# Decay of a chunked state-space scan: eight exponentials made one, bias and bound moved to GpSimd, mask moved to the cross products

## The chip, the cores and the metric

The kernel runs on one core of a Trainium2 chip. The metric is the device time of one execution in microseconds, as the median of several runs. The core has a matrix engine (TensorE, PE in the profile, whose weight loads are shown apart as PEld), a vector engine (VectorE, DVE), an engine for activation functions (ScalarE, ACT), a general engine (GpSimd, POOL) and an engine that issues transfers (SyncE, SP). Each works off its own queue in order and they meet at semaphores. PE writes its results to PSUM; the other data of the core lie in SBUF.

## The reference, cut to what matters

The reference is one layer of a streaming encoder: 1024 prompt positions and 64 sample positions go through a combined input projection, a state-space scan (SSD), differential attention, gated branches and a convolutional feed-forward part. The change lies in the scan. For one chunk, with `dtc` the step sizes, `bc` and `cc` the two projected factors and `xc` the rows, the reference computes:

```python
acum = jnp.cumsum(dtc * a_neg, axis=1)
seg = acum[:, :, None] - acum[:, None, :]
decay = jnp.exp(jnp.where(causal[None, :, :, None, None], seg, -jnp.inf))
xdt = xc * dtc[..., None]
cb = jnp.einsum('blgn,bsgn->blsg', cc, bc)
y = jnp.einsum('blsg,blsge,bsgep->blgep', cb, decay, xdt)
y = y + jnp.einsum('blgn,bgepn->blgep', cc, state) * jnp.exp(acum)[..., None]
to_end = jnp.exp(acum[:, -1:] - acum)
state = state * jnp.exp(acum[:, -1])[..., None, None] + jnp.einsum('blgn,blge,blgep->bgepn', bc, to_end, xdt)
```

There are 32 heads in 4 groups of 8. The decay differs by head (`e`), the cross products `cb` are shared by the 8 heads of a group. `a_neg` is negative, so `seg` is at most zero on the causal side.

## The kernel before, in words

The kernel holds all 1088 positions as columns and goes through these stages: input projections, attention with the rest of the input projections between its steps, the scan with branch products between its steps, the last branch product, the output projection, and the feed-forward part. The order in which each engine's queue is filled is made by a planner: the program is traced in one order, every instruction has a priority from that order, and the planner gives each engine the instruction of highest priority that it expects to be ready, by a simulated timeline of its own. Some instructions are pinned behind others by hand (`issue_after`) or raised (`high_priority`), but not those of the scan's steps.

**The step sizes** are made early, in `steps()`, while the q and k projections run. `dt_tok` is the step size, `nacum` the negative running sum of `dt * a`, `dtw` the step size times the decay to the chunk's end, each as a tile of 128 positions by 9 chunks by 32 heads. `dt_tok` and `dtw` are the two halves of one tile `dtt`. The running sums are also written, head by head as rows, to the scratch `a_sc` in DRAM.

**The scan** goes over 36 steps: 4 groups, and 9 chunks in each, 8 of 128 positions (the kernel uses 128 where the reference uses 64, which gives the same sums) and one of 64 for the sample stream. A step is cut into `front` and `back`, and `front` of the next step is traced ahead of `back` of this one. `ask` (L1284) loads the running sums of 8 heads, broadcast to all partitions, into the tile `bc` of 128 x 8 x 128; there are four such buffers.

`front` works in this order:

- ACT takes the exponential of `bc` into `e2` (L1294), twice, for the term from the old state.
- PE transposes the rows into `tr` (L1297) and makes the cross products in `cb` (L1299, L1300); ACT copies `cb` to SBUF as `b_cb` (L1302), the transposed factor in its first 128 columns and the cross products behind it.
- DVE multiplies `tr` by the two halves of `dtt` into `xx` (L1306), of which `xdt` and `xw` are the halves.
- POOL masks `bc`: it puts -1e30 where the column is before the row's position (L1307).
- ACT takes the exponential of `bc` head by head (L1309), eight instructions, since the bias `nacum` is one number per partition and head.
- DVE multiplies `bc` by the cross products (L1310).

`back` multiplies `xdt` by `bc` into `yi` on PE (L1318), the old state into `ye` (L1324); DVE joins them in `y` (L1325, L1326). PE makes the update of the state (L1330) from `b_cb` and `xw`; POOL multiplies the old state by its decay (L1335) and DVE adds the update (L1337). After each span of 384 or 320 columns `gated`, `normed` and `scaled` (L1342 to L1374) gate and normalise `y` on DVE and ACT and store it.

**Between the steps** the function `fill` traces branch products, 1.17 units a step, which keep PE's queue full: weights are loaded, cast on ACT (L155), the remainder taken on DVE (L156), three matmuls a block run on PE (L170 to L172), and the result is copied out of one of three PSUM banks (`more = psi, 1` and the two of `pm`) by ACT (L232, L970) or DVE (L234). None of these depends on the step beside which it is traced.

Of the kernel before, what the change touches and what calls it, by code (L numbers as in the profile page):

```python
# [11 lines left out]
AF = mybir.ActivationFunctionType  # L12
ALU = mybir.AluOpType
# [4 lines left out]
P = 128  # L18
# [71 lines left out]
def hybrid_layer(ctx: ExitStack, tc: tile.TileContext, xT, xt, prm, cst, rope, wvd, win, wbs, wba, wout, wup, wdn,  # L90
                 ckT, cv, st0, yT, kT, v, ssm, conv, ffn):
    nc = tc.nc
    V, S, G, PE = nc.vector, nc.scalar, nc.gpsimd, nc.tensor
    act = S.activation
# [166 lines left out]
    nacum, decs = (dq.tile([P, 9, 32], F32, name=n) for n in ("nacum", "decs"))  # L261
    dtt = dq.tile([P, 2, 9, 32], F32, name="dtt")
    dt_tok, dtw = dtt[:, 0], dtt[:, 1]
# [441 lines left out]
    def steps():  # L705
        flat = [four[:, 288 * i : 288 * (i + 1)] for i in range(3)] + [row("fx", "dt2")[:, :288]]
        da, e, t, t2 = (x.rearrange("p (a b) -> p a b", b=32) for x in flat)
# [30 lines left out]
        V.tensor_tensor(out=flat(dtw), in0=pl, in1=flat(nacum), op=ALU.add)  # L738
        act(dtw, dtw, AF.Exp)
        V.tensor_tensor(out=dtw, in0=dtw, in1=dt_tok, op=ALU.mult)  # L740
        yield
        for c, w in WIDE:
            af = row("fc", "af")[:32, :w]
# [176 lines left out]
    for at, (p, s) in enumerate(rest):  # L920
# [8 lines left out]
        if s == 1 and p in LATER:  # L929
            split_part(LATER[p], seen["copy"], seen["read"])  # L930
    beside = chain(cached_keys(), one_by_one(steps()))
    for n in range(1, len(INPUT)):
        blocks = blocks_of(n + 1) if n + 1 < len(INPUT) else None
# [331 lines left out]
    with (tc.tile_pool(name="sin", bufs=1) as sin, tc.tile_pool(name="sp", bufs=1) as sp,  # L1265
# [21 lines left out]
        def front(g, ch, o, bx, xs, bc):  # L1287
            L = P if ch < 8 else TS
            cs = slice(o, o + L)
            h8 = slice(8 * g, 8 * g + 8)  # L1290
            e2 = sp.tile([P, 4, P], F32, name="e2", tag="e2", bufs=3)
            for u in range(2):
                half = slice(64 * u, 64 * u + 64)
                act(e2[half, :, :L], bc.rearrange("p (j u) t -> p u j t", u=2)[half, u, :, :L], AF.Exp)  # L1294
            tr = psi.tile([P, 512], F32, name="tr", tag="tr")
            for j in range(4):
                PE.transpose(tr[:L, P * j : P * (j + 1)], xs[:, j, cs], ident)  # L1297
            cb = psi.tile([P, 512], F32, name="cb", tag="cb")
            PE.transpose(cb[:L, 0:P], bx[:, 0, cs], ident)  # L1299
            PE.matmul(cb[:L, P : P + L], bx[:, 0, cs], bx[:, 1, cs], start=True, stop=True)  # L1300
            b_cb = sp.tile([P, 2 * P], F32, name="b_cb", tag="b_cb", bufs=3)
            S.copy(b_cb[:L, : P + L], cb[:L, : P + L])  # L1302
            xx = sp.tile([P, 2, 8, 64], F32, name="xx", tag="xx", bufs=2)
            xdt, xw = xx[:, 0], xx[:, 1]
            tr3 = tr[:L].rearrange("p (e q) -> p e q", e=8).unsqueeze(1).to_broadcast([L, 2, 8, 64])
            V.tensor_tensor(out=xx[:L], in0=tr3, in1=dtt[:L, :, ch, h8].unsqueeze(3).to_broadcast([L, 2, 8, 64]), op=ALU.mult)  # L1306
            G.affine_select(bc[:L, :, :L], bc[:L, :, :L], [[0, 8], [1, L]], ALU.is_ge, -1e30, base=0, channel_multiplier=-1)  # L1307
            for e in range(8):
                act(bc[:L, e, :L], bc[:L, e, :L], AF.Exp, bias=nacum[:L, ch, 8 * g + e : 8 * g + e + 1])  # L1309
            V.tensor_tensor(out=bc[:L, :, :L], in0=bc[:L, :, :L], in1=b_cb[:L, P : P + L].unsqueeze(1).to_broadcast([L, 8, L]), op=ALU.mult)  # L1310
            return L, cs, bc, e2, b_cb, xdt, xw

# [65 lines left out]
        def scan():  # L1378
# [9 lines left out]
            def begin(n):  # L1388
                if n == len(steps):
                    return None  # L1390
                if n and n + 2 < len(steps):
                    asked.append(ask(*steps[n + 2]))
                i, g, c, w, o = steps[n]
                return front(g, (c + o) // P, o, *got[i], asked[n])
# [465 lines left out]
    for i in range(4 * len(DOWN)):  # L1860
        g, last = i // 4, i % 4 == 3 and i + 1 < 4 * len(DOWN)
# [125 lines left out]
```

## Time and profile before

| | us |
|---|---|
| median of 3 runs | 2413.91 |
| lowest and highest of them | 2413.68, 2415.92 |
| the profiled execution, its own time | 2411.51 |
| its span in the trace | 2409.7 |
| PE busy | 2373.4 |
| DVE busy | 1729.4 |
| ACT busy | 1201.2 |
| POOL busy | 634.4 |
| first scan step's `bc` product (L1310) starts at | 1136.3 |
| last scan step's `bc` product starts at | 1456.7 |

The profile is of one execution, taken on the core itself. The table's busy times are sums over the whole span. The granted clock of TensorE was 0.999 over the span. A row that groups instructions reads: line, engine, operation, tile written and tiles read, shapes, how many; then busy microseconds and mean nanoseconds of one; then the idle time of the engine ahead of them and whom it waited for. A row of the timeline reads: start, duration, engine, line, and how many instructions are merged in it. A row of waits reads: who waited, for whom, microseconds in all, how many times, the longest. Durations of matmuls overlap, since PE works on several at once, and spans on POOL are rough.

### The profile page before, as it was taken

The numbers are of one execution on the slowest core, as the hardware profiler recorded it, in microseconds if no ns is written. First come the engines' busy times: TensorE is split into PE (matmuls) and PEld (weight loads), VectorE is DVE, ScalarE is ACT, GpSimd is POOL, SyncE is SP. The second block draws the span as 40 slices with busy tenths as digits, with TensorE's granted clock in tenths as the row PEclk, the third lists the DMA queues.
The fourth block names the chain that finished last, engine by engine and source line by source line (L and its number), as shares of the span: only waits on it lengthen the run. The fifth ranks groups of instructions, "written<-read, shape, count | busy, mean of one in ns | idle before, by whom it ended". The sixth has DMA issues, their size and how long they took to land. (4 is left out here: it accounts for less than half of the span.)

```text
span 2409.7 us, 48636 instructions
## 1 busy us (share of the span) xinstructions
PE 2373.4 (98%) x18649; PEld 2302.2 (96%) x18649; DVE 1729.4 (72%) x2938; ACT 1201.2 (50%) x2600; POOL 634.4 (26%) x689
## 2 busy tenths in 40 slices
PE   8999999999999999999999999999999999999998
PEld 8999999999999999999898889999899999999998
DVE  4678887646858768884898886647866667677765
ACT  6444454335656656665566664334443343353442
POOL 0032443320100000001223220012254455443444
PEclk9999999999999999999999999999999999999999
DMA  7873768526554444435978956663124324357876
GB/s 246 273 245 129 266 221 303 170 102 208 160 156 161 151 144 137 148 110 188 353 266 280 331 192 205 203 215 130 65 82 164 138 98 162 127 191 211 246 184 106
DMA packets 288170, 449.74 MB, mean 187 GB/s; under 512 B 35833, under 2 KB 178306, under 8 KB 287938
## 3 DMA queue, kind: packets, MB, share of 16 engines
q1 hardware_dynamic: 258594, 387.00, 48.6%
q0 software_dynamic: 11040, 26.34, 5.4%
q10 hardware_dynamic: 18304, 33.30, 3.7%
q8 instruction: 147, 2.41, 0.4%
q14 instruction: 85, 0.70, 0.1%
HBM read 294.03 MB, written 152.50 MB: 185 GB/s over the span
## 5 line engine op out<-in xcount | busy, mean ns | idle before, releaser
L170 PE MATMUL mm<-b,w_hi 128*128 128x272 f32 x1376 | 407.7, 296 | 0.0
L171 PE MATMUL mm<-b,w_hi 128*128 128x272 f32 x1376 | 405.8, 295 | 0.0
L172 PE MATMUL mm<-b,w_lo 128*128 128x272 f32 x1376 | 403.8, 294 | 0.0
L171 PEld LDWEIGHTS mm<-b,w_hi 128*128 128x128 f32 x1376 | 259.5, 189 | 5.9 <-issue 4.1
L170 PEld LDWEIGHTS mm<-b,w_hi 128*128 128x128 f32 x1376 | 259.3, 188 | 5.3 <-issue 2.7
L172 PEld LDWEIGHTS mm<-b,w_lo 128*128 128x128 f32 x1376 | 259.0, 188 | 5.2 <-issue 4.2
L1629 PE MATMUL mx<-m,w_hi 128*128 128x272 f32 x792 | 152.3, 289 | 2.5 <-DVE hb L1667 1.3
L420 DVE TENSOR_TENSOR wh<-w_f,wh 128x512 fp32r<-128x512 f32 (+1 forms) x156 | 149.7, 960 | 0.7 <-ACT wh L419 0.7
L1629 PE MATMUL mx<-n,wh 128*128 128x272 f32 x1056 | 141.7, 288 | 1.3 <-DVE u L1656 0.9
L1629 PEld LDWEIGHTS mx<-n,wh 128*128 128x128 f32 x1056 | 135.7, 188 | 1.7 <-DVE u L1656 1.2
L1132 ACT ACTIVATE p_t<-sc,mx 128x512 f32<-128x512 f32 (+6 forms) x144 | 106.0, 739 | 59.0 <-DVE mx L1123 33.0
L1629 PEld LDWEIGHTS mx<-m,w_hi 128*128 128x128 f32 x792 | 124.4, 188 | 2.9 <-DVE hb L1667 1.5
L170 PE MATMUL mx<-b,w_hi 128*128 128x272 f32 x416 | 123.4, 297 | 1.1 <-ACT w_hi L155 0.8
L172 PE MATMUL mx<-b,w_lo 128*128 128x272 f32 x416 | 121.6, 294 | 0.0
L563 POOL TENSOR_TENSOR ws<-w_f 128x512 f32<-128x512 f32 (+1 forms) x51 | 69.0, 1354 | 195.4 <-DMA w_f<-in_wdn_dram 84.2
L171 PE MATMUL mx<-b,w_hi 128*128 128x272 f32 x416 | 120.4, 290 | 0.0
L1009 DVE SCALAR_TENSOR_TENSOR cc<-pre,par,cc 128x544 f32<-128x544 f32 (+1 forms) x144 | 111.2, 772 | 8.2 <-ACT cc L1007 6.9
L156 DVE TENSOR_TENSOR w_lo<-w_f,w_hi 128x1024 fp32r<-128x1024 f32 (+1 forms) x74 | 92.5, 1251 | 33.9 <-ACT w_hi L155 33.7
L1629 PE MATMUL mx<-m,w_lo 128*128 128x272 f32 x396 | 114.2, 289 | 0.0
L1638 ACT ACTIVATE cc<-pre,par 128x544 f32<-128x544 f32 (+1 forms) x44 | 37.2, 846 | 150.0 <-DVE pre L1673 149.1
L419 ACT CAST wh<-w_f 128x512 fp32r<-128x512 f32 (+1 forms) x156 | 95.3, 613 | 26.1 <-POOL w_f L569 6.8
L155 ACT CAST w_hi<-w_f 128x1024 fp32r<-128x1024 f32 (+1 forms) x74 | 77.6, 1049 | 56.1 <-PE mm L171 30.3
(466 smaller groups left out, 7124.8 us busy)
## 6 DMA issues: line engine op xcount, KB each, us to landing
w_f<-in_win_dram SPq DMA_DIRECT2D x40, 512.0 KB, 3.9
w_f<-in_wup_dram SPq DMA_DIRECT2D x80, 256.0 KB, 2.6
w_f<-in_win_dram SPq DMA_DIRECT2D x76, 256.0 KB, 3.2
bc<-a_sc SPq DMA_DIRECT2D x32, 512.0 KB, 7.0
b<-y_sc SPq DMA_DIRECT2D x24, 544.0 KB, 8.2
h_sc<-hb SPq DMA_DIRECT2D x44, 272.0 KB, 2.1
ht<-h_sc SPq DMA_DIRECT2D x22, 544.0 KB, 4.6
t_sc<-ht SPq DMA_DIRECT2D x22, 544.0 KB, 3.0
```

The costliest lines, as they stand in the source:

```text
L155: S.copy(hi, w)
L156: V.tensor_tensor(out=lo, in0=w, in1=hi, op=ALU.subtract)
L170: PE.matmul(ps, a_hi, b_hi, start=i == 0, stop=False)
L171: PE.matmul(ps, a_hi, b_lo, start=False, stop=False)
L172: PE.matmul(ps, a_lo, b_hi, start=False, stop=i == n - 1)
L419: S.copy(hi, src)
L420: V.tensor_tensor(out=lo, in0=src, in1=hi, op=ALU.subtract)
L563: G.tensor_tensor(out=s1, in0=q21, in1=q22, op=ALU.add)
L1009: V.scalar_tensor_tensor(cc[:, :m], pre[:, i : i + m], cw(i), cc[:, :m], ALU.mult, ALU.add)
L1132: act(p_t[:n, :nk], sc[c][:n, :nk], AF.Exp, bias=mx[:n, c : c + 1], accum_out=dst)
L1629: PE.matmul(ps, w[x][:, c], b[y][:, k], start=start and k == i == 0, stop=k == 3 and i == 2, skip_group_check=not start)
L1638: act(cc[:, :n], pre[h][:, :n], AF.Identity, bias=col(O_FB + f), scale=cw(0))
```

## The change

The exponential of `decay` keeps its argument but is put together in another way, so that one ACT instruction serves all eight heads.

- In `steps()`, after `dtw` is made, `dt_tok` is bounded from below by 1e-37, replaced by its logarithm (ACT), and added to `nacum` (DVE). The step size is thus part of the exponent: `exp(acum_l - acum_s + ln dt_s)` is the decay times the step size.
- The rows need no step size any more: `xdt` is a plain copy of `tr`, by ACT. DVE makes `xw` alone, half as many columns as before.
- The mask over `bc` (128 x 1024) goes. In its place POOL adds `nacum` and takes the minimum with `ln dt`, head by head: eight instructions of 128 x 128 with two numbers per partition each. The minimum keeps the exponent bounded where the column is before the row's position, and it changes nothing on the causal side.
- One ACT exponential of 128 x 1024 follows, without a bias.
- POOL masks the cross products in `b_cb` (128 x 128) with zeros instead, behind the exponential in the order of the trace, ahead of the DVE product (L1310), which is as before.

```diff
         act(dtw, dtw, AF.Exp)
         V.tensor_tensor(out=dtw, in0=dtw, in1=dt_tok, op=ALU.mult)
+        V.tensor_scalar_max(dt_tok, dt_tok, 1e-37)
+        act(dt_tok, dt_tok, AF.Ln)
+        V.tensor_tensor(out=nacum, in0=nacum, in1=dt_tok, op=ALU.add)
         yield
...
-            tr3 = tr[:L].rearrange("p (e q) -> p e q", e=8).unsqueeze(1).to_broadcast([L, 2, 8, 64])
-            V.tensor_tensor(out=xx[:L], in0=tr3, in1=dtt[:L, :, ch, h8].unsqueeze(3).to_broadcast([L, 2, 8, 64]), op=ALU.mult)
-            G.affine_select(bc[:L, :, :L], bc[:L, :, :L], [[0, 8], [1, L]], ALU.is_ge, -1e30, base=0, channel_multiplier=-1)
+            tr3 = tr[:L].rearrange("p (e q) -> p e q", e=8)
+            S.copy(xdt[:L], tr3)
+            V.tensor_tensor(out=xw[:L], in0=tr3, in1=dtw[:L, ch, h8].unsqueeze(2).to_broadcast([L, 8, 64]), op=ALU.mult)
             for e in range(8):
-                act(bc[:L, e, :L], bc[:L, e, :L], AF.Exp, bias=nacum[:L, ch, 8 * g + e : 8 * g + e + 1])
+                G.tensor_scalar(bc[:L, e, :L], bc[:L, e, :L], nacum[:L, ch, 8 * g + e : 8 * g + e + 1], dt_tok[:L, ch, 8 * g + e : 8 * g + e + 1], ALU.add, ALU.min)
+            act(bc[:L, :, :L], bc[:L, :, :L], AF.Exp)
+            G.affine_select(b_cb[:L, P : P + L], b_cb[:L, P : P + L], [[1, L]], ALU.is_ge, 0.0, base=0, channel_multiplier=-1)
             V.tensor_tensor(out=bc[:L, :, :L], in0=bc[:L, :, :L], in1=b_cb[:L, P : P + L].unsqueeze(1).to_broadcast([L, 8, L]), op=ALU.mult)
```

## The prediction

> **What bounds the kernel now.** I read the stretches of the span first, then who waited inside the scan, then the groups by form there. Stretches (span, PE, weight loads, DVE, ACT, POOL busy in us, then clock and DMA): what comes ahead of the scan, the scan, what comes behind it.
>
> ```profile
> span 2409.7 us, 48636 instructions
> 30.00:1128.00 1098.00, 1090.95 (x8483) 1061.68 (x8482) 781.28 (x1443) 581.74 (x1343) 185.30 (x244) 1.00 0.55 179
> 1128.00:1470.00 342.00, 338.76 (x2757) 303.35 (x2756) 284.85 (x372) 216.52 (x522) 90.78 (x68) 1.00 0.81 276
> 1470.00:2383.00 913.00, 903.06 (x7125) 897.61 (x7124) 633.24 (x1048) 375.88 (x667) 350.06 (x364) 1.00 0.53 161
> ```
>
> PE bounds it: in the scan, the only long stretch that the change touches, it stands idle for 342.00 - 338.76 = 3.2 us. Its work there is the scan's matmuls with branch products laid between them, and none of these is added or removed. So a gain in the scan can come only out of 3.2 us, while a loss has no such lid. The PE waits of the scan:
>
> ```profile
> PE yi L1318 <- ACT y L1328: 1.9, 1, 1.9
> PE tr L1297 <- DMA in<-x_sc: 0.7, 1, 0.7
> PE yi L1318 <- DVE y L1326: 0.6, 1, 0.6
> ```
>
> None is the decay tile `bc`. How much time `bc` has in hand is read from pairs: the DVE product that finishes it (L1310, start and duration) and the first matmul that reads it (L1318). First step, a tight one, last step:
>
> ```profile
> 1136.34 1.23 DVE L1310 TENSOR_TENSOR bc<-bc,b_cb 128x1024 f32<-128x1024 f32 x1 [0.34 <-ACT bc L1309]
> 1138.71 1.09 PE L1318 MATMUL yi<-bc,xx 128*64 128x128 f32 x16
> ...
> 1176.51 1.21 DVE L1310 TENSOR_TENSOR bc<-bc,b_cb 128x1024 f32<-128x1024 f32 x1
> 1178.93 1.09 PE L1318 MATMUL yi<-bc,xx 128*64 128x128 f32 x16
> ...
> 1456.71 0.67 DVE L1310 TENSOR_TENSOR bc<-bc,b_cb 64x512 f32<-64x512 f32 x1
> 1466.54 0.68 PE L1318 MATMUL yi<-bc,xx 64*64 64x64 f32 x16
> ```
>
> Slack is 1.1, 1.2 and 9.2 us here. Over all 36 pairs the middle one is 8.1; in order the short ones are 1.1, 1.2, 2.1, 2.7, 2.8, 2.9, 3.1, 3.2, 3.9, 4.1, 4.2, and then 5.1 and more. This list is the kernel's cover: growth of the chain ahead of L1310 costs nothing until it exceeds an entry.
>
> **The change part by part.** Groups of the scan, with their busy time and mean ns (the second row is one step's eight from the timeline); then two POOL and one DVE line with smallest, middle and largest duration, and that DVE line's group:
>
> ```profile
> L1309 ACT ACTIVATE bc<-bc,nacum 128x128 f32<-128x128 f32 (+1 forms) x288 | 87.2, 384 | 16.3 <-POOL bc L1307 16.0
> 1223.11 2.45 ACT L1309 ACTIVATE bc<-bc,nacum 128x128 f32<-128x128 f32 x8
> L155 ACT CAST w_hi<-w_f 128x1024 fp32r<-128x1024 f32 x17 | 17.8, 1044 | 11.3 <-PE mx L171 5.6 <-PE mm L171 5.6
> L1333 ACT COPY state<-stp 128x512 f32<-128x512 f32 x4 | 2.3, 571 | 2.9 <-PE stp L1330 2.9
> L1306 DVE TENSOR_TENSOR xx<-tr,dtt 128x1024 f32<-128x1024 f32 x32 | 38.9, 1216 | 5.3 <-PE tr L1297 3.4 <-DMA o_sc<-ol 1.8
> L1337 DVE TENSOR_TENSOR state<-state,stp 128x512 f32<-128x512 f32 x32 | 21.7, 677 | 1.3 <-PE stp L1330 1.3
> L1307 POOL TENSOR_SCALAR_AFFINE_SELECT bc<-bc 128x1024 f32<-128x1024 f32 x32 | 39.8, 1244 | 134.6 <-ACT e L1294 131.0 <-PE ye L1324 2.0 <-DMA bc<-a_sc 1.2
> L1335 POOL TENSOR_TENSOR state<-state,decs 128x512 f32<-128x512 f32 x28 | 42.3, 1512 | 96.5 <-DVE state L1337 77.4 <-ACT state L1333 17.4 <-PE ye L1324 1.8
> L1307 POOL TENSOR_SCALAR_AFFINE_SELECT bc<-bc x36: 652/1092/2132, 1130.1 to 1441.5; 128x1024 f32<-128x1024 f32 x32, 64x512 f32<-64x512 f32 x4
> L1335 POOL TENSOR_TENSOR state<-state,decs x28: 1037/1047/3618, 1140.7 to 1454.3; 128x512 f32<-128x512 f32 x28
> L1344 DVE SCALAR_TENSOR_TENSOR y<-in,par,y x48: 537/608/1500, 1153.5 to 1471.8; 128x384 f32<-128x384 f32 x32, 128x320 f32<-128x320 f32 x16
> L1344 DVE SCALAR_TENSOR_TENSOR y<-in,par,y 128x384 f32<-128x384 f32 (+1 forms) x44 | 27.6, 687 | 0.1
> ```
>
> *ACT.* The eight exponentials of a step go (87.2 us in all; 2.45 us for one step's eight, back to back). One of 128x1024 comes, 1.04 us as L155's same shape, some 36 us in all with the four half-size steps, and the copy of the plain rows from PSUM, 36 x 0.571 = 21 us as L1333. ACT is freed of some 31 us, and of 1.4 us on `bc`'s chain.
>
> *DVE.* The doubled product of 1.216 us becomes one of 512 columns from PSUM, 0.677 as L1337: 36 x 0.54 = 19 us freed.
>
> *POOL.* One mask a step (1.244 us mean) goes. Eight two-scalar instructions of 128x128 come, which the trace has nowhere, and a 128x128 mask behind them. Free time of one: on the mask's own line, (1092 - 652) / 512 = 0.86 ns a column, so 1092 - 896 x 0.86 = 0.32 us; as a two-operand instruction by L1646 below, 0.297 at 64 columns plus 64 x (1037 - 297) / 448 ns = 0.40. I take 0.32, since the form has one tensor input as the mask has. On top comes waiting beside DVE, which the rows show to go by the instruction and not by its size:
>
> ```profile
> L1646 POOL TENSOR_TENSOR hb<-hb,cc x63: 297/1220/1693, 1727.6 to 2146.8; 128x544 f32<-128x544 f32 x21, 128x480 f32<-128x480 f32 x21, 128x64 f32<-128x64 f32 x21
> L994 POOL COPY pre<-par x24: 186/188/1379, 563.7 to 1086.6; 128x3 f32<-128x3 f32 x24
> L1676 POOL COPY con<-pre x21: 643/652/710, 1733.9 to 2142.1; 128x2 f32<-128x2 f32 x21
> 1993.27 1.29 DVE L420 TENSOR_TENSOR wh<-w_f,wh 128x512 fp32r<-128x512 f32 x1
> ...
> 1993.96 0.65 POOL L1676 COPY con<-pre 128x2 f32<-128x2 f32 x1
> ```
>
> A copy of two or three columns takes 0.19 us alone and 0.65 beside DVE products from SBUF: the last two rows show it ending with the DVE instruction (1994.61 and 1994.56). In the scan the mask loses 1.244 - 1.092 = 0.15 us and L1335 1.512 - 1.037 = 0.47 us each, 0.30 over both. So eight take 8 x (0.32 + 0.30) = 5.0 us where the one took 1.24; ends 8 x 0.32 = 2.6 (no waiting) and 8 x (0.40 + 0.47) = 7.0 (all wait as L1335 or L1676). With ACT's 1.4 back, the chain to L1310 grows by 5.0 - 1.24 - 1.4 = 2.4 us; ends -0.1 and +4.3. Against the list of slack: at 2.4 the three shortest fail by 1.3 + 1.2 + 0.3 = 2.8 us of PE waiting; at 4.3 eleven fail by 16 us; at -0.1 none. PE's later matmuls slide with it, so nothing gives this back.
>
> *What waits behind.* The merged exponential stands in ACT's queue until POOL's eighth is done; behind it stand the casts of branch weights (L155), the copies out of PSUM that free the three banks (L232, L970) and the next step's exponentials. ACT waited for the mask 16.0 us so far, at no row among PE's waits; PE's one wait for ACT was 1.9 us. I take 2 us for this, ends 0 and 4. DVE's freed 19 us are met by the opposite cost: L1344's mean is 0.08 us over its middle and its largest more than twice that, which I put down to POOL, and POOL will be asked some five times as often (36 x 10 instructions instead of 68); with about 220 of the scan's 372 DVE instructions reading two SBUF tensors (36 of L1310, 48 of L1344, as many of L1362 and smaller groups) and 0.08 us more on each, 18 us come back, ends 0 and 35. So DVE stays near 285 us of 342 and I give it no gain but its one PE wait: -0.6 (end -3.2, all PE idle time of the scan). On POOL itself, L1335 queues behind the eight; POOL's sum becomes 36 x 5.0 + 36 x 0.32 + 47 = 239 us of 342, so it still has room.
>
> *The mask on the products.* It needs the ACT copy of `cb`, in POOL's in-order queue:
>
> ```profile
> 1283.11 1.24 POOL L1307 TENSOR_SCALAR_AFFINE_SELECT bc<-bc 128x1024 f32<-128x1024 f32 x1 [3.06 <-ACT e L1294]
> ...
> 1300.25 0.36 ACT L1302 COPY b_cb<-cb 128x256 f32<-128x256 f32 x1
> ```
>
> Here the old mask ran 17 us ahead of that copy. Priced at nothing as long as the planner, which orders queues by when it expects work to be ready, puts the next steps' POOL work ahead of it; if not, see the third rival.
>
> *Logarithm of dt,* once, near 217 us: a logarithm as L739, a maximum and a sum on DVE, each at most as L740, while PE runs projections that do not read it.
>
> ```profile
> L739 ACT ACTIVATE dtt<-dtt 128x288 f32<-128x288 f32 x1 | 0.4, 447 | 0.0
> L740 DVE TENSOR_TENSOR dtt<-dtt 128x288 f32<-128x288 f32 x1 | 0.7, 674 | 0.9 <-ACT dtt L739 0.9
> ```
>
> That is 1.3 us of DVE and 0.4 of ACT, once; the PSUM banks that PE has in hand cover it, and without that cover it would cost its own 1.8 us.
>
> **Sum.** -0.6 + 2.8 + 2 = +4.2 us on the profiled execution's 2411.5 (span 2409.7), so 2415.7; the median of the runs shown lies 2.4 above it, so 2418. Ends: 2413.9 - 3.2 = 2410.7 and, with 16 + 4, 2433.9. The planner orders anew whatever is not pinned, so I widen the low end to 2408.
>
> **Rivals.** *POOL and DVE take strict turns* (slower). If every one of the eight has to let one DVE product by, as L1676 does, one costs 0.32 + 0.69 (L1344's mean) = 1.01 us, a step 8.1, the chain grows by 5.5 and thirteen slacks fail by 30 us; since one stall loosens the next step I take two thirds, 2434. It decides from (342 - 47 - 12) / 36 / 8 = 0.98 us per instruction: there POOL is full. For it: L1676's 0.65 hardly varies. Against it: L1306 and L1337 alone, which read PSUM, are 38.9 + 21.7 of DVE's 284.85 us, and L1335's middle of 1.047 is its smallest, so half of its runs wait for nobody. The Trainium skill, page "SBUF — State Buffer", section "Who interferes with whom", says that a DVE instruction with two SBUF inputs and a GpSimd one that reads SBUF exclude each other for the whole instruction, which gives this rival; the trace agrees with 0.19 against 0.65 us.
>
> *More room than PE's busy time shows* (faster). PE's weight loads are busy 303.35 of 342 us, 89%, against 1061.68 of 1098, 97%, before it; 8% of 342 is 27 us, so 2387 at best if 31 us of ACT time released it.
>
> ```profile
> L1330 PE MATMUL stp<-xx,b_cb 128*128 128x512 f32 (+1 forms) x72 | 37.3, 600 | 0.0
> L1330 PEld LDWEIGHTS stp<-xx,b_cb 128*128 128x128 f32 (+1 forms) x72 | 10.9, 190 | 0.7 <-issue 0.3 <-DVE zin L1348 0.2
> ```
>
> Against it: this one group has 37.3 us of matmul for 10.9 of loads and explains 26 of the 27. So this rival is bounded by the 3.2 us of idle time and what a new order brings: 2410, and over 0.2% only by luck. The Trainium skill, page "Perfetto Trace Analysis", section "Identifying the Most-Contended Engine", judges TensorE's room by the share of LDWEIGHTS and not by matmul busy time; by it the sum would start 27 us lower.
>
> *POOL stands for `cb`* (slower). One wait as long as the 17 us above in front of the state product L1335 stops the recurrence, since L1335's successor L1324 usually follows within 10 us: some 7 us each, two or three times, 2430.
>
> **How the numbers follow.** 0.2% is 4.8 us, about what a measurement of this kernel can tell from no change. My forecast, a small loss of 0 to 8 us (2414 to 2422): 0.50, of it 0.33 inside the bound. Strict turns: 0.20. Standing for `cb`: 0.10, of it 0.03 inside. Gain: 0.20, half of it inside. Faster 0.10, same 0.33 + 0.03 + 0.10 = 0.46, slower 0.17 + 0.20 + 0.07 = 0.44. The range 2408 to 2436 takes in the ends of the sum and the middle of strict turns, and leaves a tenth on either side.
>
> **What would show it.** Right: a POOL group of 288 two-scalar instructions in the scan with smallest near 0.32 and mean near 0.6 us; one ACT exponential a step near 1.04 us, idle ahead of it for POOL well over 16 us; the DVE product from PSUM near 0.68; DVE near 285 us of the scan; a few us of PE waits at L1318 released by L1310. Wrong: a POOL mean near 1 us with POOL over 300 us busy (strict turns); POOL idle for `b_cb` L1302 (third rival); PE waits unchanged with a shorter time, or a different time with the scan as long as before, where the planner's order elsewhere decided.

## The result and the profile after

The changed kernel takes 2441.3 us (median of 4 runs, 2440.08 to 2445.27) against 2413.8 for the kernel before: a ratio of 1.0112, with a 95% interval of 1.0095 to 1.013. It is 27.5 us slower, where 4.2 were forecast, and outside the range. The profiled execution took 2440.08 us.

The span and the busy times of the changed kernel, and then its three long stretches (columns as in the prediction: PE, weight loads, DVE, ACT, POOL, clock, DMA):

```profile
span 2438.4 us, 48689 instructions
PE 2385.1 (98%) x18649; PEld 2309.9 (95%) x18649; DVE 1720.0 (71%) x2940; ACT 1171.0 (48%) x2385; POOL 899.7 (37%) x977
```

```profile
30.00:1128.00 1098.00, 1090.77 (x8480) 1061.46 (x8479) 779.90 (x1446) 581.74 (x1346) 186.50 (x244) 1.00 0.55 179
1128.00:1499.00 371.00, 349.53 (x2755) 309.52 (x2755) 276.64 (x371) 186.61 (x306) 353.69 (x356) 0.98 0.77 254
1499.00:2412.00 913.00, 905.05 (x7122) 900.10 (x7121) 634.33 (x1049) 376.24 (x667) 351.66 (x365) 1.00 0.54 161
```

The stretch ahead of the scan is as long as before (1098 us) and so is the one behind it (913 us). The scan has grown from 342 to 371 us, and that is the whole loss. In it PE stands idle for 371.00 - 349.53 = 21.5 us instead of 3.2. The other 11 us are PE's busy time, 349.53 instead of 338.76 us for as many matmuls, with a granted clock of 0.98 instead of 1.00. ACT has given up 216.52 - 186.61 = 30 us, as forecast. POOL is busy for 353.69 of the 371 us, where the forecast had 239 of 342.

The groups of the scan that the change made or touched:

```profile
L1312 POOL TENSOR_SCALAR bc<-bc,nacum,dtt 128x128 f32<-128x128 f32 x256 | 276.6, 1092 | 30.9 <-ACT e L1297 30.8
L1312 POOL TENSOR_SCALAR bc<-bc,nacum,dtt 64x64 f32<-64x64 f32 x32 | 26.5, 840 | 0.0
L1313 ACT ACTIVATE bc<-bc 128x1024 f32<-128x1024 f32 x32 | 33.9, 1058 | 70.4 <-POOL bc L1312 70.1
L1309 ACT COPY xx<-tr 128x512 f32<-128x512 f32 x32 | 18.7, 585 | 6.6 <-PE tr L1300 4.1 <-PE yi L1323 1.6 <-PE stp L1335 0.7
L1310 DVE TENSOR_TENSOR xx<-tr,dtt 128x512 f32<-128x512 f32 x32 | 21.8, 681 | 13.4 <-ACT xx L1309 13.4
L1314 POOL TENSOR_SCALAR_AFFINE_SELECT b_cb<-b_cb 128x128 f32<-128x128 f32 x32 | 13.1, 416 | 0.0
```

And the smallest, middle and largest duration on the line of the eight:

```profile
L1312 POOL TENSOR_SCALAR bc<-bc,nacum,dtt x288: 568/790/4435, 1129.8 to 1484.4; 128x128 f32<-128x128 f32 x128, 64x64 f32<-64x64 f32 x16
```

The exponential (1.058 us), the copy (0.585) and the halved product (0.681) have the sizes of the forecast. The two-scalar instruction has not: 1.092 us in the mean, not 0.62. A step's eight hold POOL for (276.6 + 26.5) / 36 = 8.4 us, not 5.0.

Who waited in the scan, first ACT and DVE, then PE:

```profile
ACT bc L1313 <- POOL bc L1312: 81.1, 26, 7.1
DVE state L1342 <- POOL state L1340: 17.1, 9, 3.9
DVE bc L1315 <- ACT bc L1313: 16.1, 10, 3.9
DVE bc L1315 <- POOL b_cb L1314: 13.3, 9, 3.3
...
PE ye L1329 <- DVE state L1342: 5.7, 5, 2.9
PE yi L1323 <- DVE y L1331: 5.2, 3, 3.1
PE cb L1302 <- ACT grs L1360: 3.4, 2, 2.5
PE tr L1300 <- DVE xx L1310: 2.5, 3, 1.2
```

ACT stands 81 us for POOL's eight, and DVE 46 us for POOL and the exponential. None of PE's waits shown is for the decay tile itself: they are for the state, the joined `y`, a copy on ACT and the rows, whose instructions stand in DVE's and ACT's queues behind the one that waits. PE's longest single stall, from each engine's timeline, in the order of the chain:

```profile
1481.58 1.06 ACT L1313 ACTIVATE bc<-bc 128x1024 f32<-128x1024 f32 x1 [7.10 <-POOL bc L1312]
1482.74 1.23 DVE L1315 TENSOR_TENSOR bc<-bc,b_cb 128x1024 f32<-128x1024 f32 x1 [1.85 <-ACT bc L1313]
1486.71 0.67 DVE L1331 TENSOR_TENSOR y<-y,yi 128x512 f32<-128x512 f32 x1
1487.53 0.87 PE L1323 MATMUL yi<-bc,xx 128*64 128x128 f32 x5 [3.11 <-DVE y L1331]
```

The exponential waits for POOL, the product of `bc` waits for the exponential, and the join of `y` that PE needs stands behind that product in DVE's queue. PE has 19 stalls of over 0.3 us in the scan, 21.3 us together. Followed back in this way, some 18 of the 21.3 us end at POOL's eight, by three ways: 8.8 us behind the product of `bc` in DVE's queue, 5.6 us behind the merged exponential in ACT's queue, and 3.6 us through the state's product on POOL. The releasers are inferred by the profile, so these shares are estimates.

### The profile page after: what moved, and what is told of

Same layout as the page of the kernel before. It is cut to its first block, busy times and chain, and to the rows that moved or that the text cites. A ratio compares the mean times of both kernels' runs of the same rounds, so it can differ in the third digit from the quotient of the medians.

```text
span 2438.4 us, 48689 instructions
## 1 busy us (share of the span) xinstructions
PE 2385.1 (98%) x18649; PEld 2309.9 (95%) x18649; DVE 1720.0 (71%) x2940; ACT 1171.0 (48%) x2385; POOL 899.7 (37%) x977
## 5 line engine op out<-in xcount | busy, mean ns | idle before, releaser
L170 PE MATMUL mm<-b,w_hi 128*128 128x272 f32 x1376 | 406.0, 295 | 0.7 <-ACT w_hi L155 0.7
L1312 POOL TENSOR_SCALAR bc<-bc,nacum,dtt 128x128 f32<-128x128 f32 (+1 forms) x288 | 303.0, 1064 | 30.9 <-ACT e L1297 30.8
L170 PEld LDWEIGHTS mm<-b,w_hi 128*128 128x128 f32 x1376 | 259.8, 189 | 6.3 <-issue 3.5
L170 PE MATMUL mx<-b,w_hi 128*128 128x272 f32 x416 | 122.2, 294 | 1.2 <-ACT w_hi L155 0.7
L1651 POOL TENSOR_TENSOR hb<-hb,cc 128x544 f32<-128x544 f32 (+2 forms) x63 | 67.1, 1079 | 133.7 <-DVE hb L1672 99.4
L565 POOL TENSOR_TENSOR w_f<-w_f,ws 128x512 f32<-128x512 f32 (+1 forms) x51 | 74.4, 1458 | 104.5 <-issue 52.9
```

Source lines behind the costliest of these rows:

```text
L170: PE.matmul(ps, a_hi, b_hi, start=i == 0, stop=False)
L565: G.tensor_tensor(out=q12, in0=q12, in1=s2, op=ALU.subtract)
L1312: G.tensor_scalar(bc[:L, e, :L], bc[:L, e, :L], nacum[:L, ch, 8 * g + e : 8 * g + e + 1], dt_tok[:L, ch, 8 * g + e : 8 * g + e + 1], ALU.a ...
```

## The experiments

Times of the kernel before beside these runs were 2413.4 to 2414.5 us. The table has what the sections below read: the median, the ratio, the time on POOL of one step's two-scalar instructions (both shapes, all of them, over 36 steps), and from 1128 us to the end of the last `yi` matmul PE's idle time, POOL's and DVE's busy time and the granted clock.

| kernel | us | ratio, 95% interval | eight on POOL, us a step | PE idle | POOL | DVE | clock |
|---|---|---|---|---|---|---|---|
| before | 2413.8 | | | 3.2 | 91 | 282 | 1.00 |
| changed | 2441.3 | 1.0095 to 1.013 | 8.4 | 21.5 | 354 | 274 | 0.98 |
| rows alone | 2420.4 | 1.0014 to 1.0047 | | 7.6 | 86 | 265 | 1.00 |
| rows, copy on DVE | 2414.6 | 0.9991 to 1.0008 | | 5.6 | 83 | 283 | 1.00 |
| POOL part alone | 2444.6 | 1.012 to 1.0152 | 8.4 | 23.4 | 353 | 303 | 0.97 |
| four and four | 2421.1 | 1.0024 to 1.0051 | 4.2 | 7.4 | 210 | 298 | 1.00 |
| six and two | 2433.9 | 1.0069 to 1.0095 | 6.3 | 14.8 | 282 | 285 | 0.99 |
| eight on DVE | 2434.9 | 1.0067 to 1.0109 | | 9.4 | 75 | 331 | 1.00 |
| unread load | 2465.5 | 1.0193 to 1.0221 | 9.0 | 33.2 | 369 | 280 | 0.94 |
| state on DVE | 2442.7 | 1.0111 to 1.0146 | 8.6 | 24.9 | 321 | 273 | 0.98 |
| two steps ahead | 2449.9 | 1.0134 to 1.0172 | 8.7 | 24.1 | 326 | 272 | 0.97 |
| rows' exponentials ahead | 2444.0 | 1.0107 to 1.0138 | 8.5 | 24.4 | 320 | 274 | 0.98 |
| mask on DVE too | 2443.0 | 1.0115 to 1.0145 | 8.8 | 21.5 | 316 | 280 | 0.98 |
| one sum, 128x1024 | 2433.7 | 1.0066 to 1.01 | | 17.4 | 164 | 296 | 1.00 |
| more fill | 2456.4 | 1.0156 to 1.0185 | 8.2 | 15.5 | 346 | 275 | 0.98 |
| four and four, copy on DVE | 2424.3 | 1.0037 to 1.0069 | 4.4 | 11.0 | 221 | 313 | 0.99 |

### The change in two parts

The rows and the logarithm alone, with the mask and the eight exponentials as before:

```diff
+            G.affine_select(bc[:L, :, :L], bc[:L, :, :L], [[0, 8], [1, L]], ALU.is_ge, -1e30, base=0, channel_multiplier=-1)
             for e in range(8):
-                G.tensor_scalar(bc[:L, e, :L], ..., ALU.add, ALU.min)
-            act(bc[:L, :, :L], bc[:L, :, :L], AF.Exp)
-            G.affine_select(b_cb[:L, P : P + L], ...)
+                act(bc[:L, e, :L], bc[:L, e, :L], AF.Exp, bias=nacum[:L, ch, 8 * g + e : 8 * g + e + 1])
```

> The changed kernel without its GpSimd part: the old mask over bc and the eight exponentials with a bias are back; ln(dt) stays in the bias, the plain rows are still copied by ScalarE and xw alone made by VectorE. Theory A (the eight GpSimd instructions fill GpSimd and set the scan's pace): as the kernel before, 2412 to 2418 us, GpSimd about 91 us busy in the scan. Theory B (the loss comes from the copy by ScalarE, the split rows and a new order of the queues): most of the 27 us stays, over 2430 us.

The POOL part alone, with the rows as before and the bound at zero:

```diff
-            S.copy(xdt[:L], tr3)
-            V.tensor_tensor(out=xw[:L], in0=tr3, in1=dtw[:L, ch, h8]..., op=ALU.mult)
+            V.tensor_tensor(out=xx[:L], in0=tr3, in1=dtt[:L, :, ch, h8]..., op=ALU.mult)
...
-                G.tensor_scalar(..., dt_tok[:L, ch, 8 * g + e : 8 * g + e + 1], ALU.add, ALU.min)
+                G.tensor_scalar(..., zero_t[:L], ALU.add, ALU.min)
```

> The kernel before with the GpSimd part alone: eight instructions of add and minimum (the minimum against a column of zeros), one exponential, the mask on the cross products; rows and dt as before. Theory A: as the changed kernel, 2435 to 2450 us, GpSimd over 90% busy in the scan. Theory B: within 8 us of the kernel before.

The POOL part alone costs 30.8 us, as much as the whole change. The rows alone cost 6.6 us, between the ranges of the two theories, where the forecast gave them nothing. So the two parts do not add; the POOL part suffices.

### The instruction by itself

Eight each of several forms at the kernel's start, where POOL has nothing else to do (DVE does work there from 2.5 us on, so the smallest of each row is taken as the free time), on a cleared tile that is filled later: two numbers per partition, one, none, a sum alone, two numbers with 64 and 256 columns, and a sum of two tensors over 256 columns.

```diff
+    for i in range(8):
+        G.tensor_scalar(probe[:, :128], probe[:, :128], s1_, s2_, ALU.add, ALU.min)
...
+    for n in (64, 256):
+        for i in range(8):
+            G.tensor_scalar(probe[:, :n], probe[:, :n], s1_, s2_, ALU.add, ALU.min)
+    for i in range(8):
+        G.tensor_tensor(out=p2, in0=p2, in1=two.unsqueeze(2).to_broadcast([P, 2, 128]), op=ALU.add)
```

> The kernel before with extra GpSimd instructions near its start, on a tile that is not yet in use: add and minimum over 128 columns with two pointers, with one pointer, with none, an add alone, then two pointers over 64 and 256 columns, and an add of two tensors with a broadcast operand over 256 columns. If the pointers are what makes 0.79 us: none 0.3 to 0.4, one 0.55, two 0.79, and 64 and 256 columns near 0.7 and 0.9. If it is the columns: the same 0.79 without pointers, 0.57 at 64 and 1.2 at 256 columns. If it is waiting beside VectorE and not the instruction: the smallest of eight with two pointers well under 0.79.

The lines of that kernel in the order above (smallest, middle and largest duration in ns):

```profile
L270 POOL TENSOR_SCALAR nacum<-nacum,decs x8: 787/788/1406, 1.2 to 8.3; 128x128 f32<-128x128 f32 x8
...
L272 POOL TENSOR_SCALAR nacum<-nacum,decs x8: 707/866/2969, 9.1 to 16.1; 128x128 f32<-128x128 f32 x8
...
L274 POOL TENSOR_SCALAR nacum<-nacum x8: 637/640/701, 19.1 to 24.2; 128x128 f32<-128x128 f32 x8
...
L276 POOL TENSOR_SCALAR nacum<-nacum x8: 530/608/616, 25.0 to 29.7; 128x128 f32<-128x128 f32 x8
...
L279 POOL TENSOR_SCALAR nacum<-nacum,decs x16: 575/1076/1219, 30.3 to 46.0; 128x64 f32<-128x64 f32 x8, 128x256 f32<-128x256 f32 x8
...
L282 POOL TENSOR_TENSOR nacum<-nacum,decs x8: 612/612/613, 47.3 to 52.2; 128x256 f32<-128x256 f32 x8
```

Free, the instruction takes 0.787 us (smallest and middle agree in the first row), against the 0.32 of the forecast and its end of 0.40. A column costs (787 - 575) / 64 = 3.3 ns, against the 0.86 that the mask's line gave; each number per partition some 0.07 us. In the changed kernel's scan the mean is 1.092, so 1.092 - 0.787 = 0.305 us come on top, about the forecast's 0.30. That all of this is waiting beside DVE is inferred, not shown.

### How much of it on POOL

Four of the eight, then six of the eight, on POOL and the others on DVE, and all eight on DVE:

```diff
-                G.tensor_scalar(bc[:L, e, :L], ...)
+                (G if e % 2 else V).tensor_scalar(bc[:L, e, :L], ...)
```

> The changed kernel with the heads split: four of the eight add-and-minimum instructions stay on GpSimd, four go to VectorE. If the eight are the cause, by their sum on GpSimd or by the length of the chain, both halve (GpSimd about 200 us in the scan, four take 4.4 us a step instead of 8.7) and most of the 27 us come back: 2413 to 2425 us, less some us for VectorE. If the cause is the other parts (copy by ScalarE, mask behind cb, order), 2435 us or more.

```diff
-                G.tensor_scalar(bc[:L, e, :L], ...)
+                (V if e in (3, 7) else G).tensor_scalar(bc[:L, e, :L], ...)
```

> The changed kernel with two of the eight two-scalar instructions on VectorE and six on GpSimd, whose busy time then is about 280 us of the scan. Theory M (a threshold: GpSimd costs nothing until it is nearly full): 2419-2424 us, as with four and four. Rival N (the loss grows with the time that the eight take in a row, long before GpSimd is full): 2426-2436 us, half way between four and four and the changed kernel.

```diff
-                G.tensor_scalar(bc[:L, e, :L], ...)
+                V.tensor_scalar(bc[:L, e, :L], ...)
```

> The changed kernel with all eight add-and-minimum instructions on VectorE, the mask on the cross products still on GpSimd. GpSimd falls to about 52 us in the scan and no longer stands in the way of VectorE. VectorE gets 288 instructions more; at an estimated 0.2 us each 58 us, so about 320 of 342 us: VectorE then sets the pace nearly everywhere, 2418 to 2440 us. If the price of an instruction on VectorE is below 0.12 us, 2412 to 2418.

With four on POOL the time is that of the rows alone; with six it is 13.5 us above that, with eight 20.9. There is no threshold at a full POOL: six cost two thirds of what eight do with POOL at 282 of 353 us. All eight on DVE lose in another way. The instruction takes 0.363 us there in the mean, not the estimated 0.2, and DVE is 331 us busy. The scan then holds 2873 matmuls instead of 2743, since more branch products fall into it, and PE stands mostly behind the scan, for the last gate (that kernel's longest PE wait after the last `yi`):

```profile
PE gst L1357 <- DVE zin L1353: 9.6, 1, 9.6
```

### The load without a reader

The kernel before, with eight instructions of that form a step that read a constant tile and write one that nobody reads; nothing else of the change is in it:

```diff
+            for e in range(8):
+                G.tensor_scalar(idle_t[:L, :L], ident[:L, :L], nacum[:L, ch, 8 * g + e : ...], dt_tok[:L, ch, 8 * g + e : ...], ALU.add, ALU.min)
             for e in range(8):
                 act(bc[:L, e, :L], bc[:L, e, :L], AF.Exp, bias=...)
```

> The kernel before, with eight two-scalar instructions a step more on GpSimd, of the changed kernel's form and shape, behind the mask and ahead of the state; they read a constant tile and write a scratch tile that nothing reads, so no exponential waits for them. What is left out is every other part of the change. Theory P (GpSimd's load): its busy time comes to 310-345 us of the scan, the masks and states stand in its queue, and the kernel takes 2428-2445 us, as the changed one does. Rival R (what costs is that ScalarE stands behind the eight, 81 us in the changed kernel): GpSimd is as full but nobody is held, 2412-2421 us. A hold-up of VectorE alone would show as its instructions with two operands in SBUF lengthened and those with one in PSUM not, with the time between the two.

It takes 2465.5 us, 51 above the kernel before and above the ranges of both theories. Its scan, two of its POOL groups and its waits:

```profile
1128.00:1518.10 390.10, 356.94 (x2727) 314.95 (x2725) 280.24 (x365) 214.79 (x522) 368.84 (x331) 0.94 0.73 241
```

```profile
L1310 POOL TENSOR_SCALAR idle<-con,nacum,dtt 128x128 f32<-128x128 f32 x241 | 279.0, 1158 | 46.4 <-DMA o_sc<-ol 28.3
L1308 POOL TENSOR_SCALAR_AFFINE_SELECT bc<-bc 128x1024 f32<-128x1024 f32 x32 | 37.3, 1167 | 1.5 <-ACT e L1295 1.5
```

```profile
ACT bc L1312 <- POOL bc L1308: 102.1, 28, 7.9
DVE state L1340 <- POOL state L1338: 28.8, 9, 9.0
...
PE yi L1321 <- DVE y L1329: 14.5, 5, 4.3
```

No exponential reads what the eight write, and yet ACT stands 102 us for POOL: for the mask, which now stands in POOL's queue behind the eight. So the load alone suffices to do harm, through what is queued behind it, and the rival that the eight cost only because the exponentials read them is out. DVE is busy for 280 us, as in the kernel before, so lengthened DVE instructions are not the cause either. The decay tile is late in this kernel too, since its mask is what is queued: the joined `y` that PE waits for longest stands, in three of the five waits, behind the product of `bc` in DVE's queue. PE's idle time is 30.0 us above before, and at a clock of 0.94 some 0.06 x 390 = 23 us more go, an estimate: together 53, where 51 were measured.

### Taking load and waits off POOL again

If POOL's sum were the bound, less on it would help. The state's product on DVE, and then, with that in each, one edit more: the front of the scan two steps ahead; the rows' exponentials of the next step issued ahead of the merged one; the mask made on DVE while the cross products are copied:

```diff
-                G.tensor_tensor(out=new.rearrange("p (e q) -> p e q", e=8), ...
+                V.tensor_tensor(out=new.rearrange("p (e q) -> p e q", e=8), ...
```

> The changed kernel with the state product (37.5 us on GpSimd in the scan) moved to VectorE. Theory A, GpSimd's sum sets the pace: GpSimd falls to about 320 us and the scan shortens by 20 to 35 us, so 2412 to 2425 us, although VectorE gets some 22 us more. Rival C (the length of one step's chain to the decay tile sets it, not GpSimd's sum): the chain of eight is as long as before, so little comes back, 2435 to 2445 us.

```diff
-BG = 8
+BG = 6
...
-            xx = sp.tile([P, 2, 8, 64], F32, name="xx", tag="xx", bufs=2)
+            xx = sp.tile([P, 2, 8, 64], F32, name="xx", tag="xx", bufs=3)
...
-            coming = begin(0)
+            coming = [begin(0), begin(1)]
...
-                now, coming = coming, begin(n + 1)
+                now = coming.pop(0)
+                coming.append(begin(n + 2))
```

> The changed kernel with the state product on VectorE, and the front of a step begun two steps ahead instead of one (three buffers for the rows; to make room, six instead of eight buffers for the operands beside the branch products). Theory C, the length of one step's chain of eight and ScalarE's standing for it: a chain of some 11 us fits in two steps of 9.5 us, so 2415 to 2428 us. Theory A, GpSimd's sum of about 320 us: no gain, 2435 to 2447 us.

```diff
-            act(e2[half, :, :L], bc..., AF.Exp)
...
+            if n + 1 < len(steps):
+                decays(n + 1)
             act(bc[:L, :, :L], bc[:L, :, :L], AF.Exp)
```

> The changed kernel with the state's product on VectorE (2442.7 us), and with one edit more: the two exponentials of the rows for the next step, which have to be done before GpSimd may overwrite those rows, are issued on ScalarE ahead of this step's merged exponential instead of behind it. Theory S (a ring: the eight wait for ScalarE's exponential of the rows, which stands behind the merged one, which waits for the eight before; with the state's product away GpSimd idles about 35 us of the scan in this ring): the idle time goes, GpSimd runs at 320 of about 335 us, and the time falls to 2420-2432 us. Rival P' (the eight's own 300 us and their hold on the others set it, and the ring is not what is late): 2437-2447 us.

```diff
-            S.copy(b_cb[:L, : P + L], cb[:L, : P + L])
+            S.copy(b_cb[:L, :P], cb[:L, :P])
+            V.tensor_tensor(out=b_cb[:L, P : P + L], in0=cb[:L, P : P + L], in1=tri[:L, :L], op=ALU.mult)
...
-            G.affine_select(b_cb[:L, P : P + L], ...)
```

> The changed kernel with the state's product on VectorE (2442.7 us, GpSimd 321 us of 355) and, besides, the mask of the cross products done on VectorE as a product with a constant triangle while they are copied out of PSUM, so that GpSimd has only the eight and never waits for the copy of the cross products. Theory Y (the waits of GpSimd for ScalarE and TensorE, some 34 us, keep it from catching up): GpSimd works on without pause, 300 of about 330 us, 2418-2430 us. Rival Z (the eight in a row, 8.4 us a step on the way from the rows to the products, are what is late): the scan stays near 350 us, 2434-2446 us.

None of the four is faster than the changed kernel, although POOL has 28 to 38 us less to do. Three lie in the ranges of the rivals C, P' and Z; two steps ahead is slower than either theory said. Their PE idle times are 21.5 to 24.9 us. What all of them keep is the eight in a row, 8.5 to 8.8 us a step. With four, six and eight on POOL the loss goes with that number (4.2, 6.3 and 8.4 us a step give 7, 20 and 28 us), and not with POOL's sum, since at a sum of 316 to 326 us these four lose no less than the changed kernel at 354. It is no law for the other kernels: the unread load loses more at 9.0 us, with the large mask of the kernel before still on POOL beside it, and two steps ahead loses 36 us at 8.7, with two buffers fewer for the operands beside the branch products. The chain of work that ended last, as the profile infers it, leads through the scan in some of these kernels. Between 1128 and 1500 us the eight are 62.9% of it with the mask on DVE and 49.8% with the rows' exponentials ahead, but 5.3% with four on POOL.

Two of the edits show why single repairs do not help. With the state's product away from POOL, PE's longest wait is for the decay tile itself, which the changed kernel does not have among its waits:

```profile
PE yi L1323 <- DVE bc L1315: 6.2, 5, 2.4
```

And the rows' exponentials, issued earlier, do not free POOL: it waits 46.8 us for them, of which 28 come ahead of the first step, against 45.4 without that edit. So that run does not test its theory of a ring.

### A cheaper instruction, and more work beside

One sum of 128x1024 with the bias as a broadcast tensor in place of the eight, the mask over `bc` as before:

```diff
+            G.affine_select(bc[:L, :, :L], bc[:L, :, :L], [[0, 8], [1, L]], ALU.is_ge, -1e30, ...)
+            G.tensor_tensor(out=bc[:L, :, :L], in0=bc[:L, :, :L], in1=nacum[:L, ch, h8].unsqueeze(2).to_broadcast([L, 8, L]), op=ALU.add)
-            for e in range(8):
-                G.tensor_scalar(bc[:L, e, :L], ...)
...
-            G.affine_select(b_cb[:L, P : P + L], ...)
```

> The changed kernel with other work on GpSimd for the same decay: the old mask over all of bc (1.1 us), then one addition of nacum with a broadcast operand over 128 x 1024 (some 1.9 us, by 0.612 us at 256 columns and 1.04 at 512), no minimum, no mask on the cross products; one exponential, ScalarE's copy and the logarithm as changed. If the eight are the cause: GpSimd about 150 us in the scan and 2408 to 2420 us, the remainder being what the rows part alone cost (2420). If merging the exponential itself or the rows is the cause, 2430 or more.

POOL is busy for only 164 us, and still 20 us are lost, some 13 more than by the rows alone. By the expectation, 2430 us or more would speak for the merged exponential or the rows as the cause; but the kernel with four and four has both and takes 2421.1 us. DVE is longer at work. Its groups in the kernel with the rows alone, and then in this one (there the first row is POOL's sum):

```profile
L1314 DVE TENSOR_TENSOR bc<-bc,b_cb 128x1024 f32<-128x1024 f32 x32 | 41.4, 1295 | 9.1 <-ACT bc L1313 5.3 <-ACT b_cb L1305 3.8
L1348 DVE SCALAR_TENSOR_TENSOR y<-in,par,y 128x384 f32<-128x384 f32 x32 | 21.4, 725 | 0.1
L1329 DVE TENSOR_TENSOR y<-ye,e 128x512 f32<-128x512 f32 x28 | 19.2, 686 | 19.3 <-PE ye L1328 13.1 <-DMA y_sc<-y 6.2
```

```profile
L1312 POOL TENSOR_TENSOR bc<-bc,nacum 128x1024 f32<-128x1024 f32 x32 | 71.7, 2243 | 1.7
L1314 DVE TENSOR_TENSOR bc<-bc,b_cb 128x1024 f32<-128x1024 f32 x32 | 50.5, 1578 | 5.7 <-ACT bc L1313 4.4 <-ACT b_cb L1305 1.3
L1348 DVE SCALAR_TENSOR_TENSOR y<-in,par,y 128x384 f32<-128x384 f32 x32 | 26.3, 881 | 0.1
L1329 DVE TENSOR_TENSOR y<-ye,e 128x512 f32<-128x512 f32 x28 | 19.1, 681 | 10.4 <-DMA y_sc<-y 5.7 <-PE ye L1328 4.7
```

The DVE instructions with two operands in SBUF are longer, by 283 and 156 ns in the mean; the one that reads PSUM is not. In all DVE has 296.3 us to do instead of 265.2, and PE's longest sums of waits are for DVE. The Trainium skill, page "SBUF — State Buffer", section "Who interferes with whom", has this rule (two SBUF inputs on DVE against a GpSimd instruction that reads SBUF), and these rows agree. Eight short POOL instructions hold DVE up as well. The same two groups in the POOL part alone:

```profile
L1313 DVE TENSOR_TENSOR bc<-bc,b_cb 128x1024 f32<-128x1024 f32 x32 | 43.8, 1368 | 16.7 <-POOL b_cb L1312 9.5 <-ACT bc L1311 6.9
L1347 DVE SCALAR_TENSOR_TENSOR y<-in,par,y 128x384 f32<-128x384 f32 x32 | 25.4, 853 | 0.0
```

There DVE is busy for 303 us, against 282 in the kernel before with the same work. That the longer DVE instructions make up the loss of the kernel with one sum is likely, but not shown: ACT also stands 45 us for POOL in it.

About an eighth more branch products inside the scan, to fill PE's idle time:

```diff
-SCAN_STEPS = 1.17
+SCAN_STEPS = 1.32
```

> The changed kernel with one constant raised, so that about an eighth more of the branch's products (1.32 instead of 1.17 units at each turn of the scan) are placed inside the scan. Theory P (GpSimd sets the pace of the scan, and what is paid is the 21.5 us in which TensorE then has nothing to do): the scan stays as long as GpSimd's 354 us or grows a little, TensorE's idle time in it falls to 5 to 12 us, and the time falls to 2424-2432 us. Rival Q (TensorE stands at the scan's own matmuls, which are late whatever is placed around them, or the products that are moved up are missing behind the scan): the idle time stays above 17 us or comes again behind the scan, 2436-2446 us.

It loses 15 us more, above the ranges of both theories. PE's idle time in the scan falls only to 15.5 us, and the products moved up are missing behind it, where PE stands for the last gate (the longest PE wait after the scan in this kernel):

```profile
PE gst L1357 <- DVE zin L1353: 13.2, 1, 13.2
```

### The copy of the rows

The rows alone, with the copy on DVE:

```diff
-            S.copy(xdt[:L], tr3)
+            V.tensor_copy(out=xdt[:L], in_=tr3)
```

> The part with the rows alone (ln of the step sizes in the bias, plain rows copied; 2420.4 us), with the copy on VectorE in place of ScalarE. Theory T (the 7 us of that part are the copies on ScalarE, which stand ahead of the copy of the cross products that TensorE waits for): ScalarE is back near 215 us, the waits of the cross products for ScalarE are gone, 2411-2417 us. Rival U (the part costs by where the order of the work falls, whichever engine copies): 2418-2425 us.

2414.6 us, the time of the kernel before. In the rows' kernel with the copy on ACT a PE wait stood that neither before nor this kernel has:

```profile
PE cb L1302 <- ACT b_cb L1305: 3.2, 3, 1.6
```

Moving the copy to DVE gives back 5.8 of the 6.6 us, so it is the copy on ACT that costs. By this row a part of it, 3.2 us, comes through the copy of the cross products, whose PSUM tile PE needs and which shares ACT's queue with it. A second way is open: the copy and DVE's product write halves of one tile, and DVE waited for the copy:

```profile
DVE xx L1310 <- ACT xx L1309: 12.8, 10, 3.9
```

Moving the copy to DVE takes away both, so the runs do not say how much each costs. Both repairs at once, four of the eight and the copy on DVE:

```diff
-            S.copy(xdt[:L], tr3)
+            V.tensor_copy(out=xdt[:L], in_=tr3)
...
-                G.tensor_scalar(bc[:L, e, :L], ...)
+                (G if e % 2 else V).tensor_scalar(bc[:L, e, :L], ...)
```

> The changed kernel with both costs found so far taken out: four of the eight two-scalar instructions on VectorE, and the plain rows copied by VectorE in place of ScalarE. ScalarE then does 31 us less than in the kernel before plus nothing, VectorE about 40 us more. Theory V (TensorE bounds the scan, so freed ScalarE time is worth nothing, and the two costs add up to the whole loss): 2411-2419 us, the time of the kernel before. Rival W (the freed time on ScalarE is worth something): under 2409 us. Rival X (VectorE, at 315 to 325 us of the scan, is now what is late): 2420-2430 us.

2424.3 us: the two savings do not add. DVE has 313 of 354 us to do, ACT only 167, and the time is in the range given for a late DVE; but half of PE's idle time is one wait for a copy on ACT (`PE mx L170 <- ACT b_g L232`, 5.7 us), so that DVE is the cause is not shown. 50 us less on ACT, with 30 us more on DVE, brought no gain here.

## Why the prediction was wrong

**What bounds the kernel** held. The stretches outside the scan did not move, the freed 30 us of ACT bought nothing, and the loss came out at PE: 18 us more idle time, and 11 us more busy time at a lower clock, a cost that the forecast did not have.

**The step that failed is the price of the two-scalar instruction**: "free time of one", 0.32 us with an end at 0.40, measured 0.787. The mask's line gave the time for a column, 0.86 ns, and the choice was made because both have one tensor input; the form costs 3.3 ns a column. The ends were taken from the mask and from a sum of two tensors, and neither bounds another kind of instruction. With 0.787 + 0.305 = 1.092 us, and 0.840 in the four half-size steps, a step's eight are 8.4 us and the chain grows by 8.4 - 1.24 - 1.4 = 5.8 us, not 2.4. In the prediction's list of slack thirteen entries are shorter than 5.8 and fail by 34 us together, so its own sum would be -0.6 + 34 + 2 = 35 us instead of 4: this one price turns a small loss into one of the order measured, 27.5 us. The prediction's own point at which POOL is full, 0.98 us per instruction, is passed at a mean of (276.6 + 26.5) / 288 = 1.05.

**Waiting beside DVE**, 0.30 us, came out at 0.305. The size was right; the agreement to 5 ns is luck, since 0.30 is the mean of 0.15 and 0.47 on two other lines. **Strict turns**, the slower rival, had the size (1.01 us an instruction, a full POOL) and the sign it gave, POOL over 300 us with a mean near 1, but not the mechanism: the instruction is slow when nothing runs beside it. Its time, 2434, was short of 2441 because a third was taken off for stalls that loosen the next step; that its undiscounted 30 us are near the 27.5 measured is luck, as its reason was wrong.

**Where the late work meets PE** was wrong too. The sum let PE wait only where a product of `bc` overran its slack, and gave 2 us (ends 0 and 4) to what stands behind. In the changed kernel no PE wait shown is for `bc`, so the forecast's sign, PE waits at `yi` released by the product of `bc`, did not come. ACT's waits for POOL rose from 16 to 81 us, and PE's stalls came through what stood behind the late instructions, in the queues of DVE, ACT and POOL. The unread load shows that such queueing alone suffices.

**DVE near 285 us**: 277 of 371. Of the 19 us freed 284.85 - 276.64 = 8 show, so 11 came back, where 18 were forecast. **The copy of the rows**, priced as ACT time only, costs some 6 us by itself, and nothing visible once POOL is what is late. **The third rival**, POOL standing for `b_cb`, did not come: POOL's mask has no idle time ahead of it. **More room than PE busy shows**: no run was faster than the kernel before.

**Not shown**: how much each of the three ways from the eight to PE costs by itself. The shares of PE's stalls above are followed back in one trace, and no edit that took one way away made the kernel faster, since another wait took its place.

## What to carry to other kernels

A kind of instruction that the trace does not have is not bounded by another kind of the same shape on that engine, above all on GpSimd: measure it alone, or let the range reach to where its engine is full. Before work is moved to an engine with idle time, ask what stands behind it in that engine's queue and in the queues of those who wait; here one step's eight in a row cost long before the engine was full. Time freed on an engine that PE did not wait for was worth nothing here, and a copy put into that engine's queue still cost by its place.

## What the runs showed of the hardware

On GpSimd a two-scalar instruction on 128x128 takes 0.787 us, more than a sum of two tensors on 128x256 with a broadcast second one (0.612 us), although the latter moves twice the columns. On VectorE the same instruction was 0.363 us in the kernel with four of the eight there.

In the changed kernel's scan TensorE's clock fell to half after some short stalls, for one or two pieces of 3.4 us. Stretches around one stall of 2.46 us (`PE cb` waiting for ACT) and behind 3 us of which PE was idle for 3.00 - 1.55 = 1.45:

```profile
1217.60:1221.00 3.40, 0.94 (x7) 0.55 (x6) 1.05 (x3) 2.14 (x4) 3.40 (x5) 1.00 0.12 36
1221.00:1224.40 3.40, 3.40 (x9) 1.88 (x9) 3.37 (x7) 2.74 (x6) 3.40 (x4) 0.51 0.77 188
1224.40:1227.80 3.40, 3.40 (x18) 3.40 (x17) 2.09 (x3) 0.93 (x2) 3.40 (x3) 0.50 0.94 292
1227.80:1231.00 3.20, 3.20 (x28) 3.20 (x28) 2.67 (x4) 3.10 (x5) 3.20 (x5) 0.99 0.57 204
```

```profile
1400.00:1403.00 3.00, 1.55 (x12) 1.19 (x11) 1.90 (x4) 2.22 (x5) 3.00 (x5) 1.00 0.72 239
1403.00:1405.40 2.40, 2.40 (x24) 1.45 (x24) 1.55 (x4) 2.37 (x6) 2.40 (x4) 0.99 0.91 223
1405.40:1408.80 3.40, 3.40 (x17) 3.40 (x16) 3.40 (x5) 2.43 (x5) 3.40 (x5) 0.50 1.07 404
```

So such a wait cost more than its length: at 0.98 over 368 us some 7 us here, at 0.94 some 23 us with the unread load (estimates from the rounded clock). Not every stall did this: in the kernel before PE was idle for 1.9 us between 1300 and 1350 us, and its clock stayed at 1.00. The Trainium skill, page "TensorE: Matmul & The Clock Gate", section "What's actually happening", gives half rate after an idle window of about 3.4 us; the pieces here have that length, but the idle time ahead of them was shorter, 2.46 and 1.45 us. What share of idle time it takes is not shown.
